# Samples' recurrence on VectorE, a joined lowest level of the prompt recurrence, and a new closing order in a two-layer decoder step

## Chip, cores and metric

The kernel runs on one NeuronCore of a Trainium2 chip. The metric is device time of one execution in microseconds (us). Before the change the median of 3 runs is 2471.2 us (2469.78 to 2472.68).

## What is computed

One inference step of a small decoder, for a prompt of 1024 tokens and a group of 8 samples of one token each. Both share all weights. Model width is 1024, there are 2 layers, and everything is float32.

- Layer 0: a gated linear recurrence (HGRN2, 4 heads, a 128 x 128 state per head) next to cross-attention into 256 memory tokens, then a SwiGLU feed-forward part. After it one shared key and value set is projected.
- Layer 1: stick-breaking attention over those keys and values next to cross-attention, then the feed-forward part.
- RMSNorm stands around every part, and the outputs are added to the residual.

The recurrence is, for each head with gate f, key k, value v and query q:

```
S_t = f_t * S_(t-1) + k_t v_t^T          (f and k scale the rows of S)
o_t = S_t^T q_t
```

For the samples this is one step from a stored state: S = f * S0 + k v^T, o = S^T q, and the new S is an output. For the prompt the 1024 steps are done in blocks: scores between keys and queries inside a block of 128 tokens, with the products of gates between them, and a carried state from block to block.

Outputs are the two residual streams, the recurrent states, the shared keys and values and the memory's keys and values.

## The kernel before

The prompt is worked in two groups of 512 tokens, and the 8 samples ride along as columns 512 to 519 of group 1. Activations stand transposed: 128 model rows by up to 520 tokens. Weights are float32 and are split into two float32r parts, high and low, so that a product takes three matmuls (lines 206, 207 and 220). Raw weights come over SyncE's queue into a ring of 5 tiles (line 201), ScalarE casts the high part, VectorE subtracts to get the low part, and the split tiles stand in another ring of 5.

Work is written as Python generators. A function `weave` draws from several of them by weights, so the recurrence of one group alternates with projections of the other. The library's scheduler then decides the order on each engine. Every engine works its own queue in order.

**Prompt recurrence** (`hgrn_prompt`, lines 1147 to 1223). For each head, line 1154 multiplies keys by queries for four chunks of 128 tokens; line 1156 keeps only the diagonal (multiply with the identity) in a tile `at`. Line 1161 multiplies the queries by their gates. Then come seven levels, m = 1, 2, 4 ... 64, over two pairs of heads. At a level, line 1174 multiplies all 128 keys of a chunk by those 64 queries that stand in the odd sub-blocks of m tokens. Lines 1179 to 1181 then bring the products of gates one level up, in place, in Q, K and F. Line 1184 copies, under a mask, the scores that belong to this level into `at`. After the levels, lines 1195 to 1222 form the state updates and the outputs. Group 0's recurrence is woven with the memory's keys and values (lines 807, 824 and 851), group 1's with the first feed-forward part of group 0.

**Samples' recurrence** (`hgrn_sample`, lines 1088 to 1145). It is woven with group 1's gate projection and the second feed-forward part of group 0. Keys and values are transposed to rows of samples (lines 1096 and 1097). For each head the old states of the 8 samples are loaded (line 1110) into a large tile (tag c, 4 buffers, 128 x 1024); a second such tile gets the values spread over a block diagonal (line 1113, with the constant `bdm`). VectorE scales the state by the gates (line 1117). TensorE forms the k v products in two halves (line 1122), which VectorE adds (line 1123). Eight small products, one for each sample, read the state out (line 1125). The new state is stored (line 1128). At the end the read-outs go through line 1134's transposes to a norm.

**Closing part** (`close` of `ffn_w`, lines 664 to 696, and `out_rows`). In the last feed-forward part of group 1 the tokens are done in two halves, so that the first half's output leaves while the second is computed: first 256 tokens (two blocks of 128 rows), then 256 tokens and the 8 samples (three blocks). For each of 8 row blocks m, line 680 multiplies, line 685 adds, lines 687 to 690 sum squares and scale. Then line 753 transposes, line 768 sums the squares, 776 and 777 make the norm, lines 782 and 785 combine with the residual, and lines 790 and 792 store.

Helpers used by the change: `split_to` (lines 226 to 228) makes high and low parts, ScalarE then VectorE; `sample_pv` (lines 938 to 950) already reads out attention values with the constant `selr`, whose slice b is a 128 x 8 matrix with ones in column b, so that a product with it sums 128 rows into output row b (line 948). `B()` is a ring of 7 tiles of 128 x 512, `S()` a ring of 3 PSUM banks.

Of the kernel before, what the change touches and what calls it, by code (L numbers as in the profile page):

```python
# [9 lines left out]
F32 = mybir.dt.float32  # L10
# [13 lines left out]
def tile_decoder(  # L24
# [550 lines left out]
    class ffn_w:  # L575
# [88 lines left out]
        def close(self, f0, nf, mids):  # L664
# [3 lines left out]
            for a in range(2):  # L668
# [4 lines left out]
                for m in range(ND):  # L673
                    if a == 0:
                        ws.append(split_w(w_down[l], f0, nf, m * P, self.spl4))
# [412 lines left out]
    def hgrn_sample(Ft, Kt, Qt, vs):  # L1088
        HB = H * NB
        kc = small([P, HB], tag="ss")  # L1090
        for h in range(H):
            nc.vector.tensor_copy(kc[:, h * NB : (h + 1) * NB], Kt[h // 2][:, h % 2, G : G + NB])
        pk = S()
        pvv = S()
        for h in range(H):
            nc.tensor.transpose(pk[:NB, h * P : (h + 1) * P], kc[:, h * NB : (h + 1) * NB], ident)
            nc.tensor.transpose(pvv[:NB, h * P : (h + 1) * P], vs[:, h, :], ident)
        kT = B()
        nc.vector.tensor_copy(kT[:NB, :512], pk[:NB, :])
        vT = B()  # L1100
        nc.vector.tensor_copy(vT[:NB, :512], pvv[:NB, :])
        po = S()
        for h in range(H):
            qd = small([P, NB, NB], tag="qd", bufs=2)
            nc.vector.tensor_mul(
                qd, sel, Qt[h // 2][:, h % 2, G : G + NB].unsqueeze(2).to_broadcast([P, NB, NB])
            )
# [5 lines left out]
            nc.vector.tensor_mul(  # L1113
                vbv[:NB], vT[:NB, h * P : (h + 1) * P].unsqueeze(1).to_broadcast([NB, NB, P]),
                bdm.to_broadcast([NB, NB, P]),
            )
            nc.vector.tensor_mul(
                stv, stv, Ft[h // 2][:, h % 2, G : G + NB].unsqueeze(2).to_broadcast([P, NB, P])
            )
            for a in range(2):  # L1120
                ps = S()
                nc.tensor.matmul(ps, kT[:NB, h * P : (h + 1) * P], vb[:NB, a, :], start=True, stop=True)
                nc.vector.tensor_add(st[:, a, :], st[:, a, :], ps)
            for b in range(NB):
                nc.tensor.matmul(
                    po[:NB, h * P : (h + 1) * P], qd[:, b, :], stv[:, b, :], start=(b == 0), stop=(b == NB - 1)
                )
# [19 lines left out]
    def hgrn_prompt(g, Ft, Kt, Qt, Vt):  # L1147
        atts = []
        for h in range(H):
            K_, Q_ = Kt[h // 2][:, h % 2, :], Qt[h // 2][:, h % 2, :]  # L1150
            pd = S()
            for c in range(CH):
                cs = slice(c * P, (c + 1) * P)
                nc.tensor.matmul(pd[:, cs], K_[:, cs], Q_[:, cs], start=True, stop=True)
# [6 lines left out]
            nc.vector.tensor_mul(Q_[:, :G], Q_[:, :G], Ft[h // 2][:, h % 2, :G])  # L1161
            yield
        for lv in range(7):
            m = 1 << lv
            nbg = G // (2 * m)
            for hp in range(2):
# [3 lines left out]
                for hh in range(2):  # L1170
                    for c in range(CH):
                        cs = slice(c * P, (c + 1) * P)
                        rhs = Q_[:, hh, cs].rearrange("p (b t m) -> p b t m", t=2, m=m)[:, :, 1, :]
                        nc.tensor.matmul(plv[:, hh, c, :], K_[:, hh, cs], rhs, start=True, stop=True)  # L1174
# [452 lines left out]
```

## Time and profile before

| what | value |
|---|---|
| median of the 3 runs | 2471.2 us |
| profiled execution's own time | 2472.22 us |
| its span in the profile | 2470.5 us |
| granted TensorE clock | 0.999 |
| VectorE busy | 1639.5 us (66%) |
| ScalarE busy | 1236.6 us (50%) |

The profile gives each engine's instructions with start and length. PE is TensorE's matmul, PEld its weight load (which runs beside matmuls), DVE is VectorE, ACT ScalarE, POOL GpSimd, SP SyncE, which issues most transfers. A line number is that of the kernel before. A matmul's length in a record includes the time until its last result is out, so the time that a run of matmuls takes is read from the start of one run to the start of the next. A group's line ends with the idle time of the engine before it and what ended that.

### The profile page before, as it was taken

The page shows a single profiled execution, that of the slowest core. Times are in us where ns is not written, and L with a number is a line of the kernel's source. Part 1 is how long each engine was busy: PE and PEld are TensorE (multiplying, and loading weights), DVE is VectorE, ACT ScalarE, POOL GpSimd, SP SyncE. Part 2 cuts the span into 40 slices and gives each one's busy share as a digit, 9 for nine tenths or more (in the row PEclk, how much of TensorE's full clock was granted, in tenths as well). Part 3 has the DMA queues.
Part 4 walks back from the last instruction along what each step waited for, and adds up shares of the span by engine and source line. Part 5 has one row for each costly group of instructions (what it writes and reads, how often), then busy time and mean ns, then how long its engine had stood idle before and what let it go on. Part 6 is the DMA issues. An engine that isn't in the chain of part 4 may idle for free.

```text
span 2470.5 us, 42287 instructions
## 1 busy us (share of the span) xinstructions
PE 2436.5 (99%) x15971; PEld 2176.6 (88%) x15971; DVE 1639.5 (66%) x2988; ACT 1236.6 (50%) x2377; POOL 184.2 (7%) x316
## 2 busy tenths in 40 slices
PE   8999999999999999999999999999999999999998
PEld 6888888877879998899999989877777888999998
DVE  5767556754788685655756685778688466755666
ACT  5437544243445554555444554555554445664445
POOL 1000101100000000111200101212000100000000
PEclk9999999999999999999999999999999999999999
DMA  6354666546745437767666649754253573465542
GB/s 188 116 167 111 156 192 160 127 134 164 212 150 154 140 120 227 201 163 183 162 196 174 193 128 274 228 150 146 91 177 117 138 199 120 139 187 145 152 143 74
DMA packets 530503, 395.29 MB, mean 160 GB/s; under 512 B 21237, under 2 KB 468802, under 8 KB 530298
## 3 DMA queue, kind: packets, MB, share of 16 engines
q1 hardware_dynamic: 501114, 312.88, 42.4%
q0 software_dynamic: 29184, 79.70, 14.0%
q8 instruction: 126, 2.06, 0.3%
q14 instruction: 79, 0.65, 0.1%
HBM read 362.69 MB, written 101.11 MB: 188 GB/s over the span
## 4 chain that ended last, share of the span: by engine, by line
PE 88%; DVE 5%; DMA 3%; issue 2%; ACT 2%; POOL 0%; SPq 0%; DVEq 0%; ACTq 0%; POOLq 0%
PE mm L220 47%; PE q L511 13%; PE q L648 9%; PE q L464 3%; PE s L1174 2%; PE mm L1042 2%; PE s L906 1%; DMA c<-in_cache_mem_v 1%; PE s L1370 1%; PE mm L824 1%; PE mm L851 1%; PE q L680 1%; PE s L875 1%; PE s L1336 1%; PE s L899 1%
## 5 line engine op out<-in xcount | busy, mean ns | idle before, releaser
L220 PE MATMUL mm<-x,ws 128*128 128x260 f32 (+1 forms) x6240 | 1119.5, 335 | 3.2 <-DVE r L657 1.7
L220 PEld LDWEIGHTS mm<-x,ws 128*128 128x128 f32 x6240 | 941.6, 188 | 127.3 <-issue 2.7
L206 ACT CAST ws<-w 128x512 fp32r<-128x512 f32 (+1 forms) x652 | 382.8, 588 | 548.9 <-PE mm L220 396.9
L207 DVE TENSOR_TENSOR ws<-w,ws 128x512 fp32r<-128x512 f32 (+1 forms) x652 | 419.2, 648 | 253.5 <-ACT ws L206 243.5
L220 PE MATMUL mm<-m,ws 128*128 128x512 f32 (+1 forms) x1344 | 280.3, 360 | 0.5 <-DVE r L400 0.5
L220 PEld LDWEIGHTS mm<-m,ws 128*128 128x128 f32 x1344 | 218.0, 188 | 37.2 <-issue 1.0
L648 PE MATMUL q<-m,ws 128*128 128x260 f32 (+1 forms) x1824 | 221.7, 282 | 0.0
L648 PEld LDWEIGHTS q<-m,ws 128*128 128x128 f32 x1824 | 218.9, 188 | 1.1 <-DVE t L534 0.3
L502 DVE TENSOR_TENSOR ws<-w,ws 128x512 fp32r<-128x512 f32 x181 | 123.9, 690 | 87.6 <-ACT ws L501 86.1
L501 ACT CAST ws<-w 128x512 fp32r<-128x512 f32 x181 | 111.8, 621 | 109.2 <-PE q L648 32.5
L511 PE MATMUL q<-x,ws 128*128 128x260 f32 (+1 forms) x1188 | 158.1, 282 | 0.0
L511 PEld LDWEIGHTS q<-x,ws 128*128 128x128 f32 x1188 | 148.6, 188 | 0.0
L511 PE MATMUL q<-y,ws 128*128 128x260 f32 x912 | 119.9, 283 | 0.4 <-ACT q L521 0.2
L511 PEld LDWEIGHTS q<-y,ws 128*128 128x128 f32 x912 | 113.7, 189 | 1.1 <-ACT q L518 0.6
L464 PE MATMUL q<-x,ws 128*128 128x260 f32 (+1 forms) x720 | 91.3, 284 | 0.3 <-DVE r L400 0.2
L464 PEld LDWEIGHTS q<-x,ws 128*128 128x128 f32 x720 | 88.4, 188 | 1.8 <-DVE r L400 0.5
L511 PE MATMUL q<-a,ws 128*128 128x260 f32 (+1 forms) x672 | 87.1, 282 | 0.0
L511 PEld LDWEIGHTS q<-a,ws 128*128 128x128 f32 x672 | 83.2, 188 | 0.0
L657 DVE TENSOR_TENSOR r<-r,q 128x260 f32<-128x260 f32 (+1 forms) x128 | 48.4, 420 | 48.8 <-PE q L648 48.8
L237 DVE TENSOR_SCALAR t<-mm 128x512 f32<-128x512 f32 (+1 forms) x58 | 40.1, 691 | 54.1 <-PE mm L220 53.8
L563 POOL COPY mk<-a 128x1 f32<-128x1 f32 x36 | 21.0, 583 | 645.6 <-ACT a L1226 393.9
L228 DVE TENSOR_TENSOR m<-t,m 128x512 fp32r<-128x512 f32 (+1 forms) x88 | 60.8, 691 | 9.5 <-ACT m L227 8.7
(358 smaller groups left out, 3038.2 us busy)
## 6 DMA issues: line engine op xcount, KB each, us to landing
w<-in_w_gu SPq DMA_DIRECT2D x297, 256.0 KB, 3.4
w<-in_w_down SPq DMA_DIRECT2D x160, 256.0 KB, 2.8
wsum<-in_w_gu POOLq DMA_DIRECT2D x72, 512.0 KB, 6.5
w<-wsum SPq DMA_DIRECT2D x104, 256.0 KB, 3.5
w<-in_w_in_a SPq DMA_DIRECT2D x80, 256.0 KB, 3.3
w<-in_w_o SPq DMA_DIRECT2D x64, 256.0 KB, 2.8
wsum<-in_w_gu POOLq DMA_DIRECT2D x24, 640.0 KB, 7.0
wsum<-wsum POOLq DMA_DIRECT2D x24, 512.0 KB, 5.8
```

Of the source, the lines that this page charges most:

```text
L206: nc.scalar.copy(ws[:, 0, :n, :], raw[:, :n, :])
L207: nc.vector.tensor_sub(ws[:, 1, :n, :], raw[:, :n, :], ws[:, 0, :n, :].bitcast(F32))
L220: nc.tensor.matmul(ps[:, a, : PW[g]], wt, xt[k][:, xi, o : o + PW[g]], start=(k == 0 and wi == 0), stop=(k == nk - 1 and wi == 2),)
L228: nc.vector.tensor_sub(dst[1], src, dst[0].bitcast(F32))
L464: ins = nc.tensor.matmul(pp[a][:, :h], wt, xt[k][:, xi, a * h : (a + 1) * h], start=(k == 0 and wi == 0), stop=(k == ND - 1 and wi == 2),)
L501: nc.scalar.copy(w[:, 0, :], src)
L502: nc.vector.tensor_sub(w[:, 1, :], src, w[:, 0, :].bitcast(F32))
L511: nc.tensor.matmul(ps[:, :h], w[:, wj, k * P : (k + 1) * P], x[:, xi, :], start=(first and k == 0 and wi == 0), stop=(k == 3 and wi == 2), ...
L648: nc.tensor.matmul(pp[a][:, :h], wt, mids[k][:, xi, a * h : (a + 1) * h], start=(k == 0 and wi == 0), stop=(k == nf - 1 and wi == 2),)
L657: nc.vector.tensor_add(d, d, pp[a][:, :h])
L1042: nc.tensor.matmul(pb[i][:, a, :], xt[k][:, xi, c * P : (c + 1) * P], ws[:, s, :], start=(k == 0 and wi == 0), stop=(k == ND - 1 and wi == 2),
L1174: nc.tensor.matmul(plv[:, hh, c, :], K_[:, hh, cs], rhs, start=True, stop=True)
```

## The change

In the samples' recurrence, the outer product k v^T is no longer a matmul. The transposed values are written to DRAM and read back for each head as a broadcast to all 128 partitions, and VectorE multiplies them by the keys, adds them to the scaled state and multiplies the new state by the queries. What is left for TensorE is the sum over 128 rows, with `selr` as weights, in high and low parts. Four of the transposes go. The sums come out with heads and samples in another arrangement, so they are written to DRAM and read back in the right one before line 1134's transposes.

In the prompt recurrence the diagonal and level m = 1 share one load of the keys: ScalarE copies the queries before the gates and the odd queries after them side by side (128 and 64 columns), and one product covers both. Levels 2 to 64 load only 128 − m keys, since the last m of a chunk have no later query at that level. At m = 32 and 64 ScalarE copies the scores in rectangles in place of the masked copy.

In the closing part the half with the samples goes first.

```diff
     def close(self, f0, nf, mids):
...
-            for a in range(2):
+            for a in (1, 0):
                 d = slice(2 * P * a, (2 * P, NG[1])[a])
...
-                    if a == 0:
+                    if a:
                         ws.append(split_w(w_down[l], f0, nf, m * P, self.spl4))

     def hgrn_sample(Ft, Kt, Qt, vs):
-        HB = H * NB
-        kc = small([P, HB], tag="ss")
-        for h in range(H):
-            nc.vector.tensor_copy(kc[:, h * NB : (h + 1) * NB], Kt[h // 2][:, h % 2, G : G + NB])
-        pk = S()
         pvv = S()
         for h in range(H):
-            nc.tensor.transpose(pk[:NB, h * P : (h + 1) * P], kc[:, h * NB : (h + 1) * NB], ident)
             nc.tensor.transpose(pvv[:NB, h * P : (h + 1) * P], vs[:, h, :], ident)
-        kT = B()
-        nc.vector.tensor_copy(kT[:NB, :512], pk[:NB, :])
         vT = B()
         nc.vector.tensor_copy(vT[:NB, :512], pvv[:NB, :])
+        vd = tc.dram_tile([NB, 512], F32, name=nm("vd"))
+        nc.sync.dma_start(vd, vT[:NB, :])
+        yield
...
         for h in range(H):
-            qd = small([P, NB, NB], tag="qd", bufs=2)
-            nc.vector.tensor_mul(
-                qd, sel, Qt[h // 2][:, h % 2, G : G + NB].unsqueeze(2).to_broadcast([P, NB, NB])
-            )
+            def col(t):
+                return t[h // 2][:, h % 2, G : G + NB].unsqueeze(2).to_broadcast([P, NB, P])
+
             st = C()
...
             vb = C()
             vbv = vb.rearrange("p a (b v) -> p (a b) v", v=P)
-            nc.vector.tensor_mul(
-                vbv[:NB], vT[:NB, h * P : (h + 1) * P].unsqueeze(1).to_broadcast([NB, NB, P]),
-                bdm.to_broadcast([NB, NB, P]),
-            )
-            nc.vector.tensor_mul(
-                stv, stv, Ft[h // 2][:, h % 2, G : G + NB].unsqueeze(2).to_broadcast([P, NB, P])
-            )
+            nc.sync.dma_start(vbv, vd[:, h * P : (h + 1) * P].partition_broadcast(P))
+            nc.vector.tensor_mul(stv, stv, col(Ft))
+            nc.vector.tensor_mul(vbv, vbv, col(Kt))
+            nc.vector.tensor_add(st, st, vb)
+            nc.sync.dma_start(st_sample[0, :, h].rearrange("b k v -> k b v"), stv)
+            nc.vector.tensor_mul(vbv, stv, col(Qt))
             for a in range(2):
-                ps = S()
-                nc.tensor.matmul(ps, kT[:NB, h * P : (h + 1) * P], vb[:NB, a, :], start=True, stop=True)
-                nc.vector.tensor_add(st[:, a, :], st[:, a, :], ps)
-            for b in range(NB):
-                nc.tensor.matmul(
-                    po[:NB, h * P : (h + 1) * P], qd[:, b, :], stv[:, b, :], start=(b == 0), stop=(b == NB - 1)
-                )
-            nc.sync.dma_start(st_sample[0, :, h].rearrange("b k v -> k b v"), stv)
-            yield
+                qs = B(F32R), B(F32R)
+                split_to(qs, vb[:, a, :])
+                for i, p in enumerate(qs):
+                    nc.tensor.matmul(
+                        po[:NB, :], selr[:, 2 * h + a, :], p,
+                        start=(h == 0 and a == 0 and i == 0), stop=(h == H - 1 and a == 1 and i == 1),
+                    )
+            yield
+        rows = B()
+        nc.vector.tensor_copy(rows[:NB, :], po[:NB, :])
+        od = tc.dram_tile([H, NB, P], F32, name=nm("od"))
+        nc.sync.dma_start(od.rearrange("h (a b) v -> (h a) b v", a=2), rows[:NB, :].rearrange("p (b v) -> p b v", v=P))
         ot = B()
-        nc.vector.tensor_copy(ot[:NB, :], po[:NB, :])
+        nc.sync.dma_start(ot[:NB, :].rearrange("p (h v) -> p h v", v=P), od.rearrange("h b v -> b h v"))

     def hgrn_prompt(g, Ft, Kt, Qt, Vt):
         atts = []
+        def decay(F_, K_, Q_, m):
...
+            nc.vector.tensor_mul(Qv[:, :, 1, :], Qv[:, :, 1, :], Fv[:, :, 0, 0:1].to_broadcast([P, nbg, m]))
+            nc.vector.tensor_mul(Kv[:, :, 0, :], Kv[:, :, 0, :], Fv[:, :, 1, 0:1].to_broadcast([P, nbg, m]))
+            nc.vector.tensor_mul(Fv[:, :, 0, 0:1], Fv[:, :, 0, 0:1], Fv[:, :, 1, 0:1])
         for h in range(H):
-            K_, Q_ = Kt[h // 2][:, h % 2, :], Qt[h // 2][:, h % 2, :]
-            pd = S()
-            for c in range(CH):
-                cs = slice(c * P, (c + 1) * P)
-                nc.tensor.matmul(pd[:, cs], K_[:, cs], Q_[:, cs], start=True, stop=True)
+            F_, K_, Q_ = Ft[h // 2][:, h % 2, :], Kt[h // 2][:, h % 2, :], Qt[h // 2][:, h % 2, :]
+            qw = [B()[:, :384].rearrange("p (c n) -> p c n", c=2) for _ in range(2)]
+            for i in range(2):
+                nc.scalar.copy(qw[i][:, :, :P], Q_[:, i * 256 : (i + 1) * 256].rearrange("p (c n) -> p c n", c=2))
+            nc.vector.tensor_mul(Q_[:, :G], Q_[:, :G], F_[:, :G])
             at = B()
-            nc.vector.tensor_mul(
-                at.rearrange("p (c t) -> p c t", c=CH), pd.rearrange("p (c t) -> p c t", c=CH),
-                ident.unsqueeze(1).to_broadcast([P, CH, P]),
-            )
+            av = at.rearrange("p (c t) -> p c t", c=CH)
+            for i in range(2):
+                odd = Q_[:, i * 256 : (i + 1) * 256].rearrange("p (c b t) -> p c b t", c=2, t=2)[:, :, :, 1]
+                nc.scalar.copy(qw[i][:, :, P:], odd)
+                pd = S()[:, :384].rearrange("p (c n) -> p c n", c=2)
+                for c in range(2):
+                    o = (2 * i + c) * P
+                    nc.tensor.matmul(pd[:, c, :], K_[:, o : o + P], qw[i][:, c, :], start=True, stop=True)
+                ai = av[:, 2 * i : 2 * i + 2, :]
+                nc.vector.tensor_mul(ai, pd[:, :, :P], ident.unsqueeze(1).to_broadcast([P, 2, P]))
+                nc.vector.copy_predicated(
+                    ai.rearrange("p c (b t) -> p c b t", t=2)[:, :, :, 1],
+                    mask[:, 0, :].unsqueeze(1).to_broadcast([P, 2, 64]), pd[:, :, P:],
+                )
+            decay(F_, K_, Q_, 1)
...
-        for lv in range(7):
+        for lv in range(1, 7):
             m = 1 << lv
+            k, nb = P - m, 64 // m
...
-                        nc.tensor.matmul(plv[:, hh, c, :], K_[:, hh, cs], rhs, start=True, stop=True)
+                        nc.tensor.matmul(
+                            plv[:k, hh, c, :], K_[:, hh, c * P : c * P + k], rhs, start=True, stop=True
+                        )
...
+                    if m >= 32:
+                        for b in range(nb):
+                            r = slice(2 * b * m, (2 * b + 1) * m)
+                            nc.scalar.copy(av[r, :, b, :], plv[r, hh, :, b * m : (b + 1) * m])
+                        continue
...
-        bdm = const.tile([NB, NB, 1], F32, name="bdm")
```

More of the change, by code (lines that the diff above doesn't have):

```diff
@@ L1160, in hgrn_prompt @@
             atts.append(at)
-            nc.vector.tensor_mul(Q_[:, :G], Q_[:, :G], Ft[h // 2][:, h % 2, :G])
             yield
-        for lv in range(7):
+        for lv in range(1, 7):
             m = 1 << lv
-            nbg = G // (2 * m)
+            k, nb = P - m, 64 // m
             for hp in range(2):
@@ L1517, in tile_decoder @@
         nc.gpsimd.tensor_tensor(pidx, pidx, iot, op=ALU.add)
-        bdm = const.tile([NB, NB, 1], F32, name="bdm")
-        nc.gpsimd.affine_select(
-            bdm.rearrange("p b o -> p (b o)"), ones[:NB, :NB], pattern=[[-1, NB]], compare_op=ALU.is_equal,
-            fill=0.0, base=0, channel_multiplier=1,
-        )
     drain(head)
```

21 lines of the change are left out of this document (9 added, 12 removed).

## The prediction

> **What bounds the kernel now.** I read the summary of the page first, then the chain of work that ended last.
>
> ```profile
> span 2470.5 us, 42287 instructions
> PE 2436.5 (99%) x15971; PEld 2176.6 (88%) x15971; DVE 1639.5 (66%) x2988; ACT 1236.6 (50%) x2377; POOL 184.2 (7%) x316
> ...
> PE 88%; DVE 5%; DMA 3%; issue 2%; ACT 2%; POOL 0%; SPq 0%; DVEq 0%; ACTq 0%; POOLq 0%
> ```
>
> TensorE is busy through 2436.5 of 2470.5 us and carries 88% of the chain. The first rule is therefore: a microsecond less on TensorE is a microsecond less of time, as long as nothing that feeds it becomes late. A busy TensorE is an average, so I then asked for the stretches in which the edited lines run (columns: stretch, its length, busy us of PE, PEld, DVE, ACT, POOL, clock, DMA share, GB/s).
>
> ```profile
> 83.64:93.06 9.42, 8.73 (x77) 8.51 (x76) 8.92 (x17) 4.61 (x10) 0.00 (x0) 1.00 0.18 57
> 93.06:107.02 13.96, 13.96 (x118) 13.51 (x118) 12.64 (x29) 6.54 (x14) 0.00 (x0) 1.00 0.51 151
> 107.02:118.04 11.02, 11.02 (x71) 9.85 (x70) 10.84 (x27) 2.53 (x5) 0.00 (x0) 1.00 0.54 153
> 118.04:161.80 43.76, 43.76 (x318) 40.74 (x316) 35.58 (x99) 13.78 (x24) 0.00 (x0) 1.00 0.53 161
> 404.80:495.00 90.20, 90.20 (x514) 78.25 (x513) 64.53 (x162) 26.49 (x48) 14.23 (x28) 1.00 0.57 137
> 526.20:607.00 80.80, 80.80 (x377) 59.54 (x375) 45.22 (x66) 30.51 (x51) 5.66 (x10) 0.98 0.56 151
> ```
>
> The first four rows are the recurrence of prompt group 0, the fifth that of group 1, the last the samples' recurrence. TensorE is full in all of them. In group 0's first 34.4 us (three rows) VectorE is nearly full too: 8.92 + 12.64 + 10.84 = 32.4 us. There a saving on TensorE has no room. In the other three rows VectorE has 8.2, 25.7 and 35.6 us to spare.
>
> **What a product costs here.** A product of plain float32 appears in the trace as two weight loads and two matmuls. I take the time per pair from the starts of neighbouring runs (columns: start, length, engine, line, operation; x is the count), because a run's length includes the drain of its last matmul.
>
> ```profile
> 83.64 1.06 PE L1154 MATMUL s<-a,a 128*128 128x128 f32 x8
> 84.53 0.60 PE L807 MATMUL ns<-ident,c 128*128 128x128 f32 x4
> ...
> 110.69 1.89 PE L1174 MATMUL s<-a,a 128*128 128x64 f32 x16
> 112.39 3.01 PE L851 MATMUL mm<-ws,memt 128*128 128x512 f32 x12
> ...
> 418.85 11.35 PE L220 MATMUL mm<-x,ws 128*128 128x512 f32 x48
> 430.03 2.23 PE L1174 MATMUL s<-a,a 128*128 128x64 f32 x19
> ...
> 696.54 1.03 PE L906 MATMUL s<-b,c 128*128 128x256 f32 x4
> 697.41 1.03 PE L875 MATMUL s<-c,a 128*128 128x256 f32 x4
> ```
>
> 128 keys by 64 queries: 1.70 us for 16, so 106 ns. 128 by 128: 0.89 for 8, 111 ns. 128 by 256: 0.87 for 4, 218 ns. The split (float32r) product with 512 columns: 11.18 for 48, 233 ns. From 128 to 256 columns the cost doubles; from 64 to 128 it hardly moves. So at 64 columns it isn't the columns that cost. The next rows say what it is:
>
> ```profile
> L1174 PEld LDWEIGHTS s<-a,a 128*128 128x128 f32 x448 | 53.4, 192 | 1.2
> ...
> L1125 PEld LDWEIGHTS s<-c,qd 128*8 128x8 f32 x64 | 5.4, 93 | 3.5 <-issue 1.9
> ...
> 2461.03 0.64 PEld L768 LDWEIGHTS ns<-ones,st 128*128 128x128 f32 x6
> ```
>
> Line 768 multiplies by one single column and still takes 0.64/6 = 107 ns: that is the load of 128 columns of weights. A load of 8 columns is recorded at 93 ns instead of 192, which is 0.83 ns less for each column dropped, or 106 ns for 128.
>
> **Lowest level joined to the diagonal (lines 1154 and 1174, level 0).** Removed for each chunk and head: one pair at 111 and one at 106. Added: one pair with 192 columns, midway between 111 and 218, so 164. That saves 53 ns a pair, on 32 pairs in a prompt group (4 heads, 4 chunks, two pairs each): **1.7 us a group**. New in front of each product are two ScalarE copies and VectorE's F multiply. The built order places group 1's four heads between runs of 17 to 48 projection products, which hide them. In group 0 the diagonal lies in the stretch where VectorE is full; VectorE's work there grows slightly (two products with the identity and two masked copies of half size in place of one and one). I take 0 gain for group 0's diagonal (between −1.7 and +1.2, if each of the eight VectorE instructions added there cost 0.15 us more than it saves).
>
> **Levels 1 to 6 load fewer keys.** Level m = 2 to 64 drops m of 128 weight columns. If the load bounds the pair and is linear, a pair saves 106 × m/128 ns, together 106 × 126/128 = 104 ns, times 32 pairs of each level: 3.3 us a group. The floor is the 64 query columns, at most half of 111 ns, reached only by m = 64. The ends are 0 (if something else than the load holds a pair at 106) and 3.3; the 93 ns row speaks for linear, but the shortest pairs may not overlap as well, so I take 80%. For group 0 levels 3 to 6 lie in the fourth row, which has room: 3.2 × 0.8 = 2.6; levels 1 and 2 count as nothing. **Group 0: −2.6. Group 1: −2.7 and the diagonal −1.7, together −4.4.** The masked copies of the two top levels go from VectorE to ScalarE in smaller pieces; ScalarE is idle for most of these rows, and VectorE, which is the narrow one, loses work.
>
> The Trainium skill, "TensorE: Matmul & The Clock Gate", section "LDWEIGHTS (loading the stationary operand)", gives a load as the number of columns over 1.2 ns, whatever the rows; the trace agrees (107 ns at 128 columns). By it the levels save their full 3.3 us a group. [...]
>
> **The samples' recurrence.** Today each head sends 2 products with 8 rows and 512 columns and 8 with 128 columns through TensorE:
>
> ```profile
> 569.74 5.91 PE L220 MATMUL mm<-x,ws 128*128 128x260 f32 x48
> 575.58 1.98 PE L1122 MATMUL s<-c,b 8*128 8x512 f32 x4
> 577.49 0.73 PE L220 MATMUL mm<-x,ws 128*128 128x512 f32 x2
> 578.16 1.91 PE L1125 MATMUL s<-c,qd 128*8 128x128 f32 x16
> 580.00 22.01 PE L220 MATMUL mm<-x,ws 128*128 128x512 f32 x94
> ...
> L948 PE MATMUL ns<-b,selr 128*8 128x512 f32 x48 | 19.5, 434 | 0.8 <-DVE b L228 0.5
> ```
>
> From 575.58 to 580.00 is 4.42 us, less two projection products at 0.233: 3.95 a head, 15.8 for four, and about 0.4 for the four key transposes (four pairs at 0.1). After the change a head has 4 float32r products, of the form of line 948: between 233 ns in a run and 19.5/48 = 406 ns alone. Three at 233 and the last at 406 make 1.1, or 4.4 in all (3.7 to 6.5), and 0.3 for waits like line 948's (0.8 for 48). **16.2 − 4.4 − 0.3: −11.5 us.**
>
> Its price is VectorE's and the queues'.
>
> ```profile
> L1117 DVE TENSOR_TENSOR c<-c,a 128x1024 f32<-128x1024 f32 x3 | 3.6, 1217 | 1.9 <-DMA c<-in_state_hgrn 1.9
> ...
> L1113 DVE TENSOR_TENSOR c<-b,bdm 8x1024 f32<-8x1024 f32 x4 | 4.8, 1210 | 0.6 <-DMA out_st_sample<-c 0.6
> ...
> L228 DVE TENSOR_TENSOR b<-c,b 128x512 fp32r<-128x512 f32 x24 | 16.3, 681 | 2.2 <-ACT b L227 2.2
> ...
> c<-in_state_hgrn SPq DMA_DIRECT2D x4, 512.0 KB, 5.4
> out_st_sample<-c SPq DMA_DIRECT2D x4, 512.0 KB, 4.9
> ...
> b<-qd SPq DMA_DIRECT2D x24, 256.0 KB, 3.7
> ```
>
> A head goes from 1217 + 1210 and two additions of 512 columns (about 681 each) to four passes of 1217 and two at 681: 3.8 to 6.2 us, +9.7 in all. The last stretch has 35.6 us free on VectorE, so they cost nothing as long as heads overlap. New transfers are the values to DRAM and back as a broadcast (the like of b<-qd, 3.7 us) and the reads' sums to DRAM and back. SyncE holds everything queued behind a waiting transfer, here weights. In the built order 144 projection products stand between the value transposes and the first head's read-out, and 108 between the last one and the transposes of line 1134: some 28 and 20 us at 233 ns for 512 columns and 122 for 260 (5.84 for 48 above), against two round trips of about 8. So I count them as nothing; without that cover each would cost its 8 us.
>
> **The closing order.** The half with the samples' rows goes first.
>
> ```profile
> 2445.79 0.42 DVE L685 TENSOR_TENSOR r<-r,q 128x256 f32<-128x256 f32 x1
> ...
> 2450.47 0.74 DVE L785 SCALAR_TENSOR_TENSOR yT<-s,rr,hT 128x512 f32<-128x512 f32 x1
> ...
> 2459.72 1.29 PEld L753 LDWEIGHTS s<-ident,r 128*128 128x128 f32 x12
> 2460.03 0.43 DVE L685 TENSOR_TENSOR r<-r,q 128x264 f32<-128x264 f32 x1
> ...
> 2466.45 0.73 DVE L785 SCALAR_TENSOR_TENSOR yT<-s,rr,c 8x512 f32<-8x512 f32 x1
> ```
>
> From the last evacuation to the last combined row it takes 5.42 us at the middle joint (two row blocks) and 7.15 at the end (three). The end becomes the short kind: −1.73. The middle, where TensorE works through the transposes and sums in order, gets the samples' 8 transposes (1.29/12 = 108 ns) and 4 pairs of sums (107): +1.3. **−0.4**; ends −1.7 (hidden in the middle) and +1.3 (the last transfer is then 512 KB and eats the end's gain).
>
> **Sum.** −2.6 − 4.4 − 11.5 − 0.4 = −18.9 us. The profiled execution took 2472.2 us, 1.7 beside its span; it lies 1.0 above the median of the runs shown (2471.2). So 2453.3 for it, **2452.3** as a median, 0.8% faster.
>
> **Rivals.** *Loads don't shrink*: the narrower key load isn't shorter, so the change doesn't do on the levels what it says. For it: no row shows a load between 8 and 128 columns. Against: 93 beside 192 ns. Then −1.7 − 11.5 − 0.4 = −13.6: 2457.6.
>
> *Heads one after another*: each head holds two of the four large tiles (tag c). If the next head's loads start only when the last one's output has landed, a head lasts 5.4 + 3.7 + 6.2 + 2.6 (split of two halves) + 4.9 = 22.8 us. The built order gives 17.0, 22.4 and 12.9 us of projections between read-outs, so TensorE would wait 5.8 + 0.4 + 9.9 = 16 us: 2468, which is no change. The same mechanism with VectorE's queue in it ends **slower**: shared with the 56% that it is busy already (45.22 of 80.8), the 6.2 become 14, a head 30.7 us, the waits 40: about 2492. It decides from a head of some 24 us, where three heads use up the 18.9. Against: the built order issues the second head's two loads ahead of the first head's output.
>
> *Everything overlaps*: group 0 takes its full 5.0, group 1 5.0, samples 12.5, the end 1.7: 2447.0.
>
> **How the numbers follow.** Forecast 0.65, loads 0.15, everything 0.10: all faster. Late heads 0.05 as no change, 0.05 as slower. Range: from 2446, where everything overlaps, to 2461, where the levels give nothing, the read-out costs its 6.5 and the joint 1.3. I call faster or slower what exceeds 0.2% (4.9 us), about what a measurement can tell: 0.90, 0.05, 0.05.
>
> **What would show it.** Pairs of level 6 at 53 to 65 ns and of level 1 at 105; the joined product near 164. The read-out in four runs of four at 233 to 280 ns, with little idle time in front. Group 0's first stretch no shorter than VectorE's busy time in it. From last evacuation to last combined row 5.4 us. I am wrong if TensorE waits in the read-out for VectorE, or for weights held behind the new transfers.

## The result and the profile after

The changed kernel takes **2454.5 us** (median of 4 runs, 2452.7 to 2459.3) beside 2471.9 for the kernel before on the same chip (4 runs, 2469.8 to 2473.2). The ratio is 0.9933, with a 95% interval of 0.9916 to 0.9951: 0.7% faster, where 2452.3 us was forecast. The profiled execution took 2454.5 us, and its span went from 2470.5 to 2452.8 us: −17.7 where the sum of the prediction was −18.9. So the total is near, but two of its four terms are not, and they err in opposite directions.

The summary of the page after, as it was shown of before (line numbers are from here on those of the changed kernel):

```profile
span 2452.8 us, 42098 instructions
PE 2413.3 (98%) x15839; PEld 2161.2 (88%) x15839; DVE 1639.9 (67%) x2987; ACT 1252.4 (51%) x2441; POOL 187.0 (8%) x315
...
PE 84%; DVE 6%; DMA 5%; issue 2%; ACT 2%; POOL 0%; SPq 0%; DVEq 0%; ACTq 0%; POOLq 0%
```

TensorE lost 23.2 us of busy time, the span only 17.7. On the chain TensorE falls from 88% to 84%, and VectorE and transfers gain 3 points: the kernel now waits a little where it did not wait before.

To see where, I compared the start of every TensorE instruction that both kernels have, and followed the difference (after minus before) through the span: −0.4 us before the recurrence, **+1.0** after group 0's recurrence (340 us), **−18.1** after the samples (680 us), −18.1 at 2400 us, −17.7 at the end. A few matmul records are missing from each trace, so such a difference is good to some 0.3 us. Between 680 and 2400 us nothing is won or lost on the whole. By steps:

| step | forecast | in the changed kernel |
|---|---|---|
| start | 0 | −0.4 |
| group 0 (levels −2.6, diagonal 0) | −2.6 | **+1.35** |
| group 1, by the times of its pairs | −4.4 | −4.8 |
| samples, what is left up to 680 us | −11.5 | **−14.3** |
| closing part | −0.4 | +0.4 |
| sum | −18.9 | −17.7 |

**Group 0.** The first stretches of group 0's recurrence, in the view by windows (columns: stretch, length, busy us of PE, PEld, DVE, ACT, POOL, granted clock, DMA share, GB/s):

```profile
83.27:92.65 9.38, 6.03 (x29) 5.23 (x27) 7.39 (x19) 5.33 (x15) 0.00 (x0) 0.82 0.17 53
92.65:102.81 10.16, 9.60 (x71) 9.17 (x71) 9.37 (x26) 5.11 (x14) 0.00 (x0) 1.00 0.22 59
```

Before, TensorE was busy through 8.73 of the first 9.42 us. Now it stands for 3.3 us of 9.4, VectorE has 2 us to spare, and the granted clock has fallen to 0.82. That is a mean. In finer stretches the clock is at 0.50 for 3.4 us and at 1.00 on either side:

```profile
85.31:88.72 3.41, 0.63 (x4) 0.42 (x4) 2.91 (x8) 2.07 (x7) 0.00 (x0) 1.00 0.26 77
88.72:92.13 3.41, 3.07 (x10) 2.98 (x11) 2.12 (x6) 1.47 (x6) 0.00 (x0) 0.50 0.02 5
92.13:95.50 3.37, 2.72 (x20) 2.26 (x19) 3.08 (x9) 1.27 (x4) 0.00 (x0) 1.00 0.00 0
```

The timeline of TensorE names what it stands for (in brackets: idle time before the row, and what ended it):

```profile
83.27 1.47 PE L1168 MATMUL s<-b,a 128*128 128x192 f32 x8
84.57 0.60 PE L807 MATMUL ns<-ident,c 128*128 128x128 f32 x4
87.77 0.63 PE L807 MATMUL ns<-ident,c 128*128 128x128 f32 x4 [2.60 <-DVE memt L228]
89.06 2.93 PE L1168 MATMUL s<-b,a 128*128 128x192 f32 x8 [0.66 <-ACT b L1164]
91.78 0.78 PE L807 MATMUL ns<-ident,c 128*128 128x128 f32 x4
93.02 0.51 PE L824 MATMUL mm<-memt,ws 128*128 128x256 f32 x2 [0.46 <-ACT memt L227]
```

After the first head's joined products and a set of the memory's transposes, the next in TensorE's queue is a second set of transposes, which must wait until the split of the first set has emptied its bank. In the kernel before, 20 pairs of the next heads' diagonals stood between the two sets; they needed only keys and raw queries, and the wait was 0.69 us:

```profile
84.97 1.95 PE L1154 MATMUL s<-a,a 128*128 128x128 f32 x16
87.61 0.68 PE L1154 MATMUL s<-a,a 128*128 128x128 f32 x4 [0.69 <-DVE a L241]
88.12 0.60 PE L807 MATMUL ns<-ident,c 128*128 128x128 f32 x4
```

The joined product needs its copied operand, so the built order puts it behind. When the second head's eight pairs come in the changed kernel, they take 2.72/8 = 340 ns each instead of the 162 of the first eight (1.30/8): they run at half the clock, which costs 1.4 us on top of the 3.2 us of added idle time.

**Group 1's joined product and the levels** (starts of neighbouring runs):

```profile
404.76 1.46 PE L1168 MATMUL s<-b,a 128*128 128x192 f32 x8
405.93 4.23 PE L220 MATMUL mm<-x,ws 128*128 128x512 f32 x17
...
463.44 3.95 PE L1188 MATMUL s<-a,a 128*112 128x64 f32 x40
467.19 0.93 PE L220 MATMUL mm<-m,ws 128*128 128x512 f32 x3
...
474.91 2.57 PE L1188 MATMUL s<-a,a 128*96 128x64 f32 x32
477.41 7.21 PE L220 MATMUL mm<-m,ws 128*128 128x512 f32 x30
...
484.55 1.15 PE L1188 MATMUL s<-a,a 128*64 128x64 f32 x16
485.62 0.66 PE L1210 MATMUL s<-ident,a 128*128 128x128 f32 x4
```

The joined pair takes 1.17/8 = 146 ns (forecast 164). A pair with 112 keys takes 94 ns, with 96 keys 78, with 64 keys 67; 106 × keys/128 would be 93, 80 and 53. So the load is linear in its columns down to 96 keys, and level 6 stops at 67 ns.

**Samples' recurrence:**

```profile
543.51 1.09 PE L1119 MATMUL s<-b,selr 128*8 128x512 f32 x4
544.43 11.26 PE L220 MATMUL mm<-x,ws 128*128 128x512 f32 x48
557.43 5.98 PE L220 MATMUL mm<-x,ws 128*128 128x260 f32 x48 [1.73 <-DVE t L237]
```

The read-out is 0.92 us for four, 230 ns each. One wait is new: 1.73 us for VectorE. It was named in the prediction as a sign of being wrong; e2 and e9 say more on it.

**The end.** Last evacuation (line 685) and last combination (line 785) of the changed kernel:

```profile
2443.23 0.42 DVE L685 TENSOR_TENSOR r<-r,q 128x256 f32<-128x256 f32 x1
...
2447.91 0.75 DVE L785 SCALAR_TENSOR_TENSOR yT<-s,rr,hT 128x512 f32<-128x512 f32 x1
```

That is 5.43 us, as forecast (2443.23 to 2448.66), 1.72 less than before. But from there to the end of the span it is now 4.14 us (2452.8 − 2448.66), where it was 3.32 (2470.5 − 2467.18): the last transfer is now a row block of 512 KB (in the trace its last packet ends 2.3 us after the last combination; before, 1.4). And the middle joint costs 1.3, as forecast: the difference is −18.1 ahead of it and −16.8 at the last evacuation (2443.23 − 2460.03). −0.9 + 1.3 is the +0.4 of the table.

### The profile page after: what moved, and what is told of

Its sections match the earlier page's. It is cut to its first block, busy times and chain, and to the rows that moved or that the text cites. A ratio compares the mean times of both kernels' runs of the same rounds, so it can differ in the third digit from the quotient of the medians.

```text
span 2452.8 us, 42098 instructions
## 1 busy us (share of the span) xinstructions
PE 2413.3 (98%) x15839; PEld 2161.2 (88%) x15839; DVE 1639.9 (67%) x2987; ACT 1252.4 (51%) x2441; POOL 187.0 (8%) x315
## 4 chain that ended last, share of the span: by engine, by line
PE 84%; DVE 6%; DMA 5%; issue 2%; ACT 2%; POOL 0%; SPq 0%; DVEq 0%; ACTq 0%; POOLq 0%
PE mm L220 44%; PE q L511 13%; PE q L648 9%; PE q L464 3%; PE mm L1042 2%; PE s L1188 1%; DMA c<-in_cache_mem_v 1%; PE s L1385 1%; PE s L906 1%; PE mm L824 1%; PE mm L851 1%; PE q L680 1%; PE s L1351 1%; PE s L875 1%; DVE ws L207 1%
## 5 line engine op out<-in xcount | busy, mean ns | idle before, releaser
L563 POOL COPY mk<-a 128x1 f32<-128x1 f32 x36 | 21.3, 592 | 645.5 <-ACT a L1241 392.9
```

## Experiments

Two theories stood against each other for group 0. *Queue*: TensorE stands because the joined product's operand comes late, so that other work, itself waiting, moves ahead of it. *VectorE*: the stretch has more VectorE work than before, and no order helps. For the rest: does the new read-out alone give the samples' gain, what is the closing order worth, and is there a floor under a short pair? Differences below are read like those above, against the profile of before at the same TensorE instruction.

### e1: the lowest level joined in group 1 only

```diff
+        if g:
             for h in range(H):
...
+        else:
+            for h in range(H):
+                K_, Q_ = Kt[h // 2][:, h % 2, :], Qt[h // 2][:, h % 2, :]
+                pd = S()
...
-        for lv in range(1, 7):
+        for lv in range(1 if g else 0, 7):
```

> The changed kernel with the joined lowest level in prompt group 1 alone; group 0 has the old diagonal and seven levels, with the shorter key loads. Queue theory: in group 0 the joined product stands behind a ScalarE copy, a VectorE multiply and a second ScalarE copy while VectorE is nearly full; TensorE waited there, its clock fell (0.82 between 83 and 93 us) and it lost some 6 us, so this kernel gains 3 to 4.5 us on the changed one (about 2450.5) and the clock in that stretch is back at 1.00. Rival, VectorE simply full: whatever the form, its work sets the length of the first stretch of group 0; then this kernel is within 1 us of the changed one (2454.5).

Measured: 2458.4 us (2454.1 to 2461.3, 6 runs), ratio 0.9936 (0.9924 to 0.9949). Group 0 came out at −2.2 (from −0.05 to −2.26), and its stretch is full, at full clock:

```profile
83.27:92.65 9.38, 8.70 (x76) 8.37 (x75) 8.58 (x16) 4.62 (x10) 0.00 (x0) 1.00 0.18 58
```

So the stall belongs to the join in group 0, and the levels alone are worth 2.2 there: close to the 2.6 forecast, although the stretch was thought to have room for four of six levels only. The time, though, misses the 2450.5 us that the queue theory promised, and the rival's 2454.5 too. The kernel keeps a lead of 3.4 us on the changed one up to 1560 us (−21.9 beside −18.5) and then loses it, in two places: 4.0 us between 1560 and 1600 us (to −17.8) and 2.5 by 1960 us (to −15.4). The first loss begins with a wait for layer 1's stored keys; see e9 and e11.

### e2: no join at all, levels and the rest as changed

```diff
-                    nc.tensor.matmul(pd[:, c, :], K_[:, o : o + P], qw[i][:, c, :], start=True, stop=True)
+                nc.tensor.matmul(pd[:, cs], K_[:, cs], Q_[:, cs], start=True, stop=True)
...
-        for lv in range(1, 7):
+        for lv in range(7):
```

> The changed kernel without the joined level in either group; the shorter key loads stay. Queue theory: group 0 as in the run with the join in group 1 alone, and group 1 loses the 2.0 us that the joined pairs save there (155 ns in place of 217, 32 pairs): 2 us over that run, 2 us below the changed kernel. Rival, VectorE simply full: group 0 as in the changed kernel, 2 us over the changed kernel.

Measured: 2458.2 us in one run, which is not the 2 us below the changed kernel that was expected: it loses 3.0 us near 1473 us and 5.2 near 1563, each time to a wait and a half clock after it (see e11). Up to there the trace bears the theory out. Group 0 −2.1, as in e1. At 680 us it stands at −20.8, 0.9 behind e1 instead of 2.0. The join's TensorE gain in group 1 is 2.0 by the pairs' times, but part of it goes to the wait for VectorE in the samples' stretch: TensorE is idle for 1.27 us in front of a projection in e1 and 1.73 in the changed kernel, and not at all in e2 or e3, which have no join. In the other kernels with the join this wait came to 1.4 us at most. It does not come from the amount of VectorE's work: between 540 and 560 us VectorE is busy for 19.6 us in e2 and 20.0 in e3, where nothing waits, and for 16.0 in the changed kernel. What in the built order brings it stays open.

Two things follow. Without the join, group 1's levels and the samples can be read apart: −3.0 from 340 to 520 us and −15.9 from there to 680. And with no join at all this kernel stands 2.7 us ahead of the changed one at 680 us: up to there the joined level, in both groups together, was a loss.

### e3: the samples' recurrence alone

The kernel before, with `hgrn_sample` of the changed kernel:

```diff
-                nc.tensor.matmul(ps, kT[:NB, h * P : (h + 1) * P], vb[:NB, a, :], start=True, stop=True)
-                nc.vector.tensor_add(st[:, a, :], st[:, a, :], ps)
...
+            nc.vector.tensor_mul(vbv, vbv, col(Kt))
+            nc.vector.tensor_add(st, st, vb)
```

> The kernel before with the samples' recurrence of the change alone. TensorE theory: the old products took 18.6 us of TensorE's time from start to next start, the new ones take 3.7, and one wait of 1.7 us stays: 13 to 14.5 us less than before. Rival, as forecast: 11.5 less, the rest of the changed kernel's gain between group 1 and the memory attention being group 1's.

Measured: 2461.0 us in one run. From +1.3 before the samples to −14.6 after: **−15.9** alone, as in e2, more than the 11.5 forecast and than the theory's 13 to 14.5. With the wait of 1.7 us it is about the −14.3 of the changed kernel. At the end only −11.2 is left, after the longest of the waits near 1560 us (3.83 us, see e11).

Where the surplus comes from stands in the trace of *before*, around its first head:

```profile
530.00:540.00 10.00, 10.00 (x39) 5.85 (x38) 7.23 (x10) 2.10 (x4) 0.00 (x0) 0.83 0.62 179
```

```profile
532.56 1.80 PE L1125 MATMUL s<-c,qd 128*8 128x128 f32 x8
534.29 2.01 PE L220 MATMUL mm<-x,ws 128*128 128x512 f32 x4
536.23 1.04 PE L1125 MATMUL s<-c,qd 128*8 128x128 f32 x8
```

The clock granted in these 10 us was 0.83 (0.50 from 532.66 to 536.08 us, 1.00 otherwise), and four projection products took 1.94/4 = 485 ns each instead of 233, with TensorE busy all the time. Head by head, less the projection products at 233 ns between them, the old read-out took 5.8, 4.2, 3.95 and 4.2 us: 18.2. The prediction had taken the third head, the cheapest, for all four (15.8). With four transposes (0.4) and a read-out of 0.92 in place of 1.1 this gives 18.6 − 3.7 = 14.9 of the 15.9; the last microsecond I have not traced.

### e4: the closing order of before

```diff
-            for a in (1, 0):
+            for a in range(2):
...
-                    if a:
+                    if a == 0:
                         ws.append(split_w(w_down[l], f0, nf, m * P, self.spl4))
```

> The changed kernel with the old closing order. Joint theory: what the end gains with two row blocks instead of three, the middle joint pays with the samples' transposes and sums, so the span is within 0.6 us of the changed one (2452.8), with the middle 1.3 shorter and the end 1 to 1.7 longer. Rival, end alone counts: 1.7 us longer.

Measured: 2452.9 us in one run, span 2451.0. The span is 1.8 us below the changed kernel's and not within 0.6, but 1.4 of that is there before the closing part begins. From −19.5 at 2430 us to −19.5 at the end: the old order has no joint cost and no end gain. The new one goes from −18.1 to −17.7. So the new order is 0.4 us worse; e10 repeats this.

### e5: the odd queries made by VectorE straight into the joined operand

```diff
+            for i in range(2):
...
+                nc.vector.tensor_mul(qw[i][:, :, P:], odd, fod)
             nc.vector.tensor_mul(Q_[:, :G], Q_[:, :G], F_[:, :G])
...
-                nc.scalar.copy(qw[i][:, :, P:], odd)
```

> The changed kernel, but VectorE multiplies the odd queries by their gates straight into the joined operand, ahead of the multiply of all queries; the second ScalarE copy goes, and VectorE gets 16 small multiplies more. Chain theory (the wait comes from the three links copy, multiply, copy): the joined products of group 0 start earlier, and 1.5 to 4 us of the 6 lost there come back, though VectorE has more to do. Rival, VectorE's queue: with 8 more instructions of about 0.3 us in group 0 the stretch gets longer, 1 to 2 us over the changed kernel.

Measured: 2454.0 us (2452.3 to 2459.1, 4 runs), ratio 0.9916 (0.9895 to 0.9937). Group 0 is at +1.4, no better, and the 1.5 to 4 us of the chain theory did not come back. The profile shows why in part. The second wait (0.66 us, for the copy) is gone, so the chain did get shorter. But the first wait is the same 2.60 us for the split of the memory's transposes: a shorter chain does not change what stands next in TensorE's queue. And in this execution the clock stayed at 0.50 for twice as long:

```profile
89.25:96.06 6.81, 6.32 (x24) 5.35 (x23) 5.47 (x16) 2.31 (x8) 0.00 (x0) 0.50 0.01 2
```

By my estimate that costs another 1.7 us (half of the added 3.4), so the time of group 0 here does not tell what the shorter chain is worth by itself.

### e6: a probe of short pairs

```diff
-            k, nb = P - m, 64 // m
+            k, nb = {16: 8, 32: 32}.get(m, P - m), 64 // m
+            nq = {16: 8, 64: 32}.get(m, 64)
```

> The changed kernel with other shapes at three levels, so that part of the scores is left out: at m = 16 the product has 8 keys and 8 queries, at m = 32 it has 32 keys and 64 queries, at m = 64 it has 64 keys and 32 queries (the changed kernel has 112 by 64, 96 by 64 and 64 by 64, at 94, 79 and 67 ns a pair). Floor theory: a pair of load and matmul doesn't go below some 62 to 67 ns, so all three take 60 to 67. Load theory (columns over 1.2 plus a fixed 14): 21, 53 to 55 (its queries bound it) and 67. Columns theory (the 64 queries and a fixed part bound the pair): the last with 32 queries falls to 53 or less.

The run took 2452.6 us; it is there for the times of its pairs. The levels m = 16, 32 and 64 of group 1 on TensorE's timeline:

```profile
461.50 0.95 PE L1189 MATMUL s<-a,a 128*8 128x8 f32 x32
462.38 1.43 PE L220 MATMUL mm<-m,ws 128*128 128x512 f32 x5
...
471.02 2.13 PE L1189 MATMUL s<-a,a 128*32 128x64 f32 x32
473.08 7.18 PE L220 MATMUL mm<-m,ws 128*128 128x512 f32 x30
480.20 1.12 PE L1189 MATMUL s<-a,a 128*64 128x32 f32 x16
481.25 0.66 PE L1214 MATMUL s<-ident,a 128*128 128x128 f32 x4
```

8 keys by 8 queries take 0.88/32 = 27.5 ns a pair, 32 keys by 64 queries 64 ns, 64 keys by 32 queries 66 ns; 64 by 64 took 67. So there is no floor of 60 ns under every pair: the smallest goes far below. But 64 columns on either side hold a pair at 64 to 67 ns, where 0.83 ns a column gives 53. What holds it there, while 96 columns take 78, stays open. It is worth 0.4 us a group (32 × 14 ns).

The Trainium skill, "TensorE: Matmul & The Clock Gate", section "Back-to-back issue gap", gives about 62 ns for 1 to 64 columns where the instruction is decoded in software, and about 25 ns where it is not. The trace speaks for the second (27.5 ns a pair), so the 62 ns do not explain the measured 64 to 67.

### e7: the operands one head ahead

If the queue theory holds, the remedy is not a shorter chain but an earlier one, so that the second head's products stand before the second set of transposes:

```diff
+            if h == 0:
+                ready.append(operands(0))
+            if h + 1 < H:
+                ready.append(operands(h + 1))
+            qw = ready[h]
```

where `operands` holds the two ScalarE copies and the multiply of queries by gates.

> The copies and the multiply of queries by gates are issued one head ahead of the joined products, in both groups; everything else is the changed kernel. Queue theory (TensorE stands still in group 0 because the second head's joined product reaches the front of its queue before ScalarE and VectorE have made its operand): the built order now has the second head's eight pairs ahead of the second set of memory transposes, so TensorE's idle time between 83 and 103 us falls from about 4 us to under 1.5, the granted clock there comes back from 0.82 to 0.97 or more, and group 0 ends at -1 to -3 us against the kernel before instead of +1.35: 2 to 4 us below the changed kernel's time. Rival (VectorE has more work in this stretch, and the order matters little): idle time stays at 3 us or more, group 0 stays between +0.5 and +1.5, and the time within 1 us of the changed kernel.

Measured: **2451.7 us** (2449.9 to 2455.3, 5 runs), ratio 0.9918 (0.9905 to 0.9932), 3.0 us below the changed kernel on the same chip (e9). The intervals of the two overlap, but the traces show the mechanism:

```profile
83.27:92.65 9.38, 7.19 (x44) 5.96 (x43) 8.63 (x22) 6.19 (x18) 0.00 (x0) 1.00 0.18 58
92.65:102.81 10.16, 10.16 (x84) 9.82 (x83) 8.80 (x25) 3.92 (x9) 0.00 (x0) 1.00 0.27 82
```

```profile
85.11 0.60 PE L807 MATMUL ns<-ident,c 128*128 128x128 f32 x4
85.55 1.85 PE L1179 MATMUL s<-b,a 128*128 128x192 f32 x8
88.32 0.63 PE L807 MATMUL ns<-ident,c 128*128 128x128 f32 x4 [0.92 <-DVE memt L228]
89.61 1.59 PE L1179 MATMUL s<-b,a 128*128 128x192 f32 x8 [0.66 <-ACT b L1163]
```

Eight joined pairs now stand between the two sets of transposes, the waits sum to 2.0 us instead of 3.9, and the clock stays at 1.00. Group 0 comes out at −1.8 (0.17 to −1.64) instead of +1.35. Some 1.9 us of the gain is idle time and some 1.4 the clock. The idle time fell to 2.0 and not under the 1.5 that I had expected. VectorE's work is the same as in the changed kernel, so the VectorE theory is out. But e1, with the old diagonals in group 0, came to −2.2 there: even with its operands ahead, the join brings group 0 nothing of what its pairs save.

### e8: join in group 1 only, with the old closing order

The edits of e1 and e4 together.

> Joined lowest level in group 1 only, and the closing order of the kernel before. Queue theory: up to 1500 us it stands 3 to 4 us ahead of the changed kernel, as the kernel with group 1 joined alone did, and the old closing order adds 0 to 0.4. If the loss of that kernel near 1590 us (a wait of 3 us for the stored keys of layer 1, in a stretch where the transfers fill the queues) is a matter of one execution, the median comes to 2450.5 to 2452. Rival (a kernel that arrives there earlier waits longer, so what is saved before is given back): the wait is 3 us or more again and the median 2454 to 2457, no better than the changed kernel.

Measured: 2457.3 us (2456.6 to 2458.8, 5 runs), ratio 0.9938 (0.9925 to 0.9952). Group 0 −2.3, as in e1; 3.6 us ahead of the changed kernel at 680 us, as expected, but only 1.5 at 1500; −19.9 at 1560 us, then the wait for layer 1's keys again (2.65 us), −16.4 at 1600. These come near the rival's numbers (3 us or more, 2454 to 2457); but see the next.

### e9: the changed kernel once more

No edit.

> The changed kernel once more, unedited, beside the two others on one chip. Theory that the wait for layer 1's stored keys near 1585 us varies from execution to execution: in this profile it differs from the 1.0 us of the first profile by over 0.5 us, and the runs spread over 4 us or more. Rival (it follows from the kernel's timing): 1.0 us within 0.3 again. Group 0's stall, which comes from the built order, is the same in both: TensorE busy about 6.0 us of the 9.4 from 83.3 us, clock 0.82. Time 2452.5 to 2457.

Measured: 2454.7 us (2451.5 to 2455.7, 5 runs), ratio 0.9925 (0.9911 to 0.9938). Group 0 +1.3, TensorE busy 6.12 us of the 9.38, clock 0.82: the same stall. And the same wait near 1560 us, so my theory of chance is out. The wait for VectorE in the samples' stretch did differ, 0.52 us in place of 1.73, and the step from 340 to 680 us is −20.0 in place of −19.1. The wait near 1560 us in the first profile of the changed kernel, then in this one:

```profile
1561.40 1.14 PE L1351 MATMUL s<-a,a 128*128 128x128 f32 x4 [1.01 <-DMA a<-ksc]
```

```profile
1560.58 1.14 PE L1351 MATMUL s<-a,a 128*128 128x128 f32 x4 [0.89 <-DMA a<-ksc]
```

### e10: operands ahead, old closing order

The edits of e7 and e4 together.

> The operands one head ahead, and the closing order of the kernel before. Theory of the closing part (the new order costs the middle joint about as much as it saves at the end): against the operands-ahead kernel the part from 2440 us to the end changes by 0.2 us at most to the better, so the time is 2451 to 2452 unless the wait for layer 1's stored keys near 1560 us grows. Rival (the new order is worth the forecast 0.4 us or more): 0.4 us or more slower from 2440 us on. On that wait: if it is tied to which closing order is built, it is 2 us or more here, as it was with the old closing order before (2.19, 2.65), and the median goes to 2453 to 2455; if not, 0.9 to 1.0 as with the operands ahead.

Measured: 2451.5 us (2450.2 to 2454.7, 5 runs), ratio 0.9919 (0.9905 to 0.9932). The closing part goes from −20.8 at 2430 us to −20.8 here and from −20.9 to −20.5 in e7: the new order is 0.4 us worse, as in e4. The rows of its end, and its span:

```profile
2439.22 0.43 DVE L685 TENSOR_TENSOR r<-r,q 128x264 f32<-128x264 f32 x1
...
2445.65 0.73 DVE L785 SCALAR_TENSOR_TENSOR yT<-s,rr,c 8x512 f32<-8x512 f32 x1
```

```profile
span 2449.7 us, 42095 instructions
```

7.16 us to the last combination, but then only 3.3 to the end, as before. The wait near 1560 us is 1.12 us, so it does not hang on the closing order.

### e11: join in group 1 only, once more

No edit to e1.

> The kernel that joins the lowest level in group 1 only, once more. Theory that the longer wait for layer 1's stored keys near 1560 us belongs to this built kernel: 3.1 us again within 0.5, the loss of some 4 us between 1560 and 1600 us again, median 2456 to 2460. Rival (it differs from one execution to the next): a wait that differs from 3.1 by over 1 us, and a profile that keeps its lead of over 3 us on the changed kernel to the end, 2451 to 2454.

Measured: 2456.5 us (2452.1 to 2461.5, 5 runs), ratio 0.9937 (0.9923 to 0.9951). e1 and then this run:

```profile
1560.13 1.16 PE L1367 MATMUL s<-a,a 128*128 128x128 f32 x4 [3.08 <-DMA a<-ksc]
```

```profile
1560.36 1.20 PE L1367 MATMUL s<-a,a 128*128 128x128 f32 x4 [3.35 <-DMA a<-ksc]
```

The wait belongs to the built kernel: 0.62 us before, 0.89 to 1.12 in the changed kernel and with the operands ahead, 2.2 to 3.8 in the others, and the same again when a kernel is run again. It is not that whoever comes earlier waits longer: e7 and e10 arrive 21.3 and 21.5 us early and wait about 1 us, e3 arrives 14.6 us early and waits 3.83. The transfers are full ahead of it (a DMA share of 0.85 to 1.08 in slices of 20 us from 1480 to 1560 us, in the kernel before, the changed one, e5, e7, e8 and e9). Which difference of the builds decides stays open.

What follows the wait costs as well. In e1, right behind it:

```profile
1561.12:1564.51 3.39, 3.39 (x12) 2.56 (x11) 3.01 (x7) 1.26 (x2) 0.00 (x0) 0.50 0.94 324
```

So the 4.0 us that e1 loses there are 2.5 of longer wait and 1.6 of half clock. All runs that wait 2.65 us or more at this place (e1, e2, e3, e5, e6, e8, e11) then run at half clock, and those that wait 2.19 or less (before, changed, e4, e7, e9, e10) do not. Behind a wait of some 2.1 us near 1693 us the clock halves once more in e1, e8 and e11. This is part of why e1 and e8, better by more than 1 us up to 1560 us, end no better than the changed kernel; the rest of what e1 loses by 1960 us I have not traced.

## Why the prediction was right, and where it was wrong

- **Which engine decides: right.** TensorE's time is the measure, the change takes 23.2 us of it, and from 680 to 2400 us the lead is carried unchanged. That it is carried was luck for this build: of what they had at 680 us, e3 and e6 lost 3 to 4 us and e1, e2, e5, e8 and e11 5 to 7, to waits and half clocks that the prediction had no term for. None of the rivals came: loads do shrink, and heads overlap (four read-outs with no wait of their own).
- **Group 0, −2.6: the step that failed.** It came to +1.35. The levels gave their 2.2 (e1, e2, e8, e11: −2.1 to −2.3). The diagonal, counted as 0 between −1.7 and +1.2, cost about 3.5. I priced VectorE's added instructions because VectorE looked full. What counted was the queue: the old diagonals needed nothing and filled a wait of the memory's transposes, the joined ones are ready later, so the wait became visible and the clock fell to half. The sentence that TensorE is full in all the quoted stretches overlooked this place: the first row has 8.73 of 9.42 us, and the rest is the wait of 0.69. The criterion that I gave, a stretch no shorter than VectorE's busy time, could not have shown this: VectorE has 2 us to spare in it. My question for a wait that is added, who is queued around it, was asked for SyncE's queue and not for TensorE's.
- **Group 1, −4.4: right** by the pairs' times (−2.8 and −2.0), and for the levels by e2 (−3.0). The joined pair is shorter than taken (146 to 161 ns for 164), the levels are the 80% and a bit more (2.8 of 3.3). What was not seen is that with the join a wait for VectorE comes some 140 us later (up to 1.73 us), which takes back part of the join's 2.0.
- **Samples, −11.5: mechanism right, mis-sized.** It is −15.9 alone and −14.3 with the new wait (−15.2 in e9, where that wait is shorter). The old read-out was 18.2 us and not 15.8, because a cheap head stood for all and the clock of 0.98 in a quoted row was passed over: it hid 3.4 us at half clock in the first head. The read-out is 0.92 and not 1.1 a head. The transfers' round trips cost nothing visible, as argued. The sign of being wrong, a wait for VectorE, came in part: 1.73 us, in front of a projection and not of a read-out.
- **Closing, −0.4: wrong in sign, within its own ends.** The end becomes 1.72 shorter up to the last combination, as forecast, and gives 0.8 back to the longer last transfer, which I had named as an end of the range and not put into the sum; the joint costs 1.3, as forecast. From 2430 us to the end the new order comes to +0.4 in the changed kernel, e7 and e9, the old one to 0.0 in e4 and e10.
- **The total was near** because group 0's 4 us too little gain and the samples' 2.8 us too much nearly cancel. That is luck.

## What to carry to other kernels

Before an operand is rebuilt for a cheaper matmul, ask what stands next in TensorE's queue when the operand is not there yet: work without dependences that fills another's wait is worth more than its length, and preparing the operand one step ahead gave back 3.1 of the 3.5 us here. Price a repeated block from all of its repetitions, and read a granted clock below 1 in a stretch as time that the change may win back or lose; ask for finer stretches then, since a mean of 0.98 over 81 us, or of 0.82 over 9, hid 3.4 us at half clock. Measure a change by its difference along the trace as well as at the end, since another place may take the gain for a reason of its own.

## What the runs showed of the hardware

- The clock fell to half after a short idle time. TensorE stood for 2.60 us, then 0.66 (busy for 0.63 of 3.41 us), the clock was 0.50 for the next 3.41 us, and the eight pairs that ran then took 340 ns in place of 162. With waits of 0.92 and 0.66 (e7) it stayed at 1.00. The Trainium skill, "TensorE: Matmul & The Clock Gate", part 1 on the clock gate, speaks of an idle window of some 3.4 us; here less than that in one piece was enough.
- The length of one wait does not decide alone: behind 2.19 us near 1562 us (e4) the clock stayed at 1.00, behind 2.12 us near 1693 us (e1) it halved. Half clock lasted 3.4 us in most places, 6.8 in e5 (group 0) and e2 (near 1563 us).
- In the kernel before, the clock was 0.50 from 532.66 to 536.08 us with TensorE busy all the time (line 1122's products with 8 rows stand just ahead). The products with 8 rows of the other three heads show no such drop, so these rows do not tell why.
- A plain float32 pair takes 27.5 ns at 8 by 8, 64 to 67 ns with 64 columns on either side, 78 at 96 keys and 105 at 126.
